# A seven-product down-projection whose combined weights are all prepared during the up-projection

## The chip, the cores and the metric

The kernel runs on one core of a Trainium2 chip. The metric is the device time of one execution in microseconds (us). In the text PE is TensorE, ACT ScalarE, DVE VectorE, POOL GpSimd, and SP the engine that issues most DMAs.

## The reference

One layer of a diffusion backbone over 2048 tokens of width D = 1024 (batch 1): a mixer (an FNet branch and a gated recurrence, merged and projected), then a gated feed-forward network with a 3x3 depthwise convolution, then a final RMS norm. All is float32. The part that matters here is the feed-forward network, D_FF = 2816, on a grid of 32 rows by 64 columns:

```python
def conv_ffn(h, w_up, conv_w, conv_b, w_down, rows, cols):
    z = (h @ w_up).reshape(b, rows, cols, 2 * D_FF)
    z = lax.conv_general_dilated(z, conv_w, ..., padding='SAME', feature_group_count=2 * D_FF)
    z = z.reshape(b, l, 2 * D_FF) + conv_b
    return (jax.nn.silu(z[..., :D_FF]) * z[..., D_FF:]) @ w_down
...
x = x + mx[:, :, 5] * conv_ffn(h2, ffn_up, ffn_conv_w, ffn_conv_b, ffn_down, rows, GRID_W)
return rmsnorm(x, final_g)
```

## The kernel before

Every float32 product is made of three matmuls in the type fp32r: each operand is split into a high part (a cast on ACT, line 102) and a low part (operand minus high part, on POOL or DVE, line 103), and high x high, high x low and low x high are added in PSUM. `split` does this for a tile, and all splits carry the lines 102 and 103, so tiles tell them apart.

The program is written as one stream; a scheduler puts the instructions of each engine in an order, and each engine works through its own in that order. `tc.issue_after(x)` makes what is issued within it stand behind x. A tile pool with `bufs=n` gives a tile name n buffers; the next use of a buffer waits until its last reader is done.

**Up-projection** (1656 to 2687 us of the profile). `NF` = 22 pairs of column blocks, so 44 iterations, counted by jt = 2j + half. Each loads and splits its block of `ffn_up` (`load_w`, tile w_up), and makes 96 matmuls into z, a 128 x 2048 tile in PSUM; two z tiles (za, zb), which take turns, fill the PSUM. Then ACT makes the convolution's centre (line 1031) and a scaled copy `be` (line 1034), on odd iterations also the Silu (line 1036); DVE makes seven taps of the convolution (line 1063, reading z, which it frees at its end); POOL adds `be` (line 1039), and on odd iterations multiplies by the gate (line 1048); SP stores the result as dZ.

**Down-projection** (from 2687 us). The 2816 rows of `w_down` and the output's 2 x 2 blocks (halves of tokens, halves of columns) are treated as a 2 x 2 by 2 x 2 block product, done with seven products in place of eight. `PRODUCTS` says for each which one or two blocks of tokens (dZ), and which one or two of weights, are added or subtracted to make its operands, and to which output quarters the result is added. Each product has KH = 11 steps; a step needs a token operand g (128 x 1024, split in two) and a weight operand w (128 x 512, split), and makes 8 x 3 matmuls. `operand(idx)`, called AHEAD = 5 steps before the step's use, loads and prepares them: token blocks into rg, sum on DVE (line 1132), split into g; weight blocks into rv, sum on DVE (line 1136), split into w. At a product's end its last steps are done accumulator by accumulator, and each accumulator is added by DVE to its quarters of x (`evict`, line 1212). The g tiles and the quarters of x live in slots H0 to H7.

Two kinds of work for the down-projection are written into the up-projection: `gated_weights` (22 times: ffn_down times the gate vector m5, on POOL, line 1071, stored as dV) at jt 4 to 25, and `first_weights` (11 times: the weight operands of the first product; combined on POOL, line 1079, split from ws into wsr, a single buffer, and stored as dW, line 1082) at jt 28 to 38. These are places in the program's text; nothing ties them to the engines' work of those iterations. In the profile the instructions of line 1082 lie between 1826 and 1917 us. The weights of the other six products are loaded from dV, combined and split during the down-projection.

Of the kernel before, what the change touches and what calls it, by code (L numbers as in the profile page):

```python
# [26 lines left out]
P = 128  # L27
# [67 lines left out]
class Layer:  # L95
# [79 lines left out]
    def scratch(self):  # L175
# [15 lines left out]
        self.dW = [dr.tile([P, 2, TB], F32R, name=f"dW{k}") for k in range(KH)]  # L191
# [807 lines left out]
    def phase3(self, p5):  # L999
# [3 lines left out]
        self.m5 = p5.tile([P, D], F32, name="m5")  # L1003
        nc.sync.dma_start(self.m5, self.dm5)
        for j in range(NF):
            acc = []
            for half in range(2):
                jj = j + half * NF
                wh, wl = self.load_w(a["ffn_up"][0, :, jj * P:(jj + 1) * P], f"up{jj}")
                if jj == NF:  # L1010
                    self.psB.__exit__(None, None, None)
                    self.psB = tc.tile_pool(name="ps2b", bufs=1, reuse_waits="tile", space=PSUM)
                    self.zb = self.psB.__enter__()
# [8 lines left out]
                if 4 <= jt < 4 + NF:  # L1022
                    self.gated_weights(p5, jt - 4)
                elif 28 <= jt < 28 + KH:
                    self.first_weights(p5, jt - 28)
# [6 lines left out]
                if not end:  # L1032
                    be = p5.tile([P, SEQ], F32, name="be", tag="be", bufs=2)
                    nc.scalar.activation(be, z, AF.Copy, scale=self.cw[:, 7, jj:jj + 1])  # L1034
# [3 lines left out]
                if not end:  # L1038
                    nc.gpsimd.tensor_tensor(ac[:, :SEQ - 64], ac[:, :SEQ - 64], be[:, 64:], op=ADD)  # L1039
# [25 lines left out]

    def gated_weights(self, p5, k):
# [7 lines left out]
    def first_weights(self, p5, k):  # L1074

        nc = self.nc
        raw = p5.tile([P, 2, TB], F32, name="ws", tag="ws", bufs=2)
        self.load_terms(raw, self.weight_terms(PRODUCTS[0], k))
        nc.gpsimd.tensor_tensor(raw[:, 1, :], raw[:, 1, :], raw[:, 0, :], op=SUB)
        w = p5.tile([P, 2, TB], F32R, name="wsr", tag="wsr", bufs=1)  # L1080
        self.split(w[:, 0, :], w[:, 1, :], raw[:, 1, :])
        nc.gpsimd.dma_start(self.dW[k], w)
# [21 lines left out]
    def weight_terms(self, prod, k):  # L1104
        return [self.dV5[KH * r + k][:, c * TB:(c + 1) * TB] for r, c, _ in prod[1]]

    def load_terms(self, t, terms):

        for q, src in zip((1, 0), terms):
            self.nc.sync.dma_start(t[:, q, :], src)  # L1110

    def operand(self, idx):
# [4 lines left out]
        prod = PRODUCTS[p]  # L1117
        q = idx - 8
        if q % 2 == 0:
            tag = "H2" if q == 0 else "H1" if q == 2 else ("H3", "H6", "H7", "H2")[(q // 2 - 2) % 4]  # L1120
# [3 lines left out]
        rg = self.p6.tile([P, 2, 2 * TB], F32, name="rg", tag="rg", bufs=3)  # L1124
        self.load_terms(rg, [self.dZ[KH * kh + k][:, 2 * th * TB:2 * (th + 1) * TB] for th, kh, _ in prod[0]])
        if p == 0:
            nc.gpsimd.dma_start(w, self.dW[k])
        else:
            rw = self.p6.tile([P, 2, TB], F32, name="rv", tag="rv", bufs=3)
            self.load_terms(rw, self.weight_terms(prod, k))  # L1130
        if len(prod[0]) == 2:
            nc.vector.tensor_tensor(rg[:, 1, :], rg[:, 1, :], rg[:, 0, :], op=prod[0][1][2])  # L1132
        self.split(g[:, 0, :], g[:, 1, :], rg[:, 1, :])
        if p:
            if len(prod[1]) == 2:
                nc.vector.tensor_tensor(rw[:, 1, :], rw[:, 1, :], rw[:, 0, :], op=prod[1][1][2])
            self.split(w[:, 0, :], w[:, 1, :], rw[:, 1, :])
# [11 lines left out]
    def down(self, last, pools):  # L1149
# [4 lines left out]
        with ExitStack() as es:  # L1154
# [27 lines left out]
            def store(th, c, i):  # L1182
                ti = 8 * th + i
                nc.sync.dma_start(self.out[ti * P:(ti + 1) * P, c * TB:(c + 1) * TB], X[th, c][:, i, :])
# [43 lines left out]
            load_quarter(0, 1, "H4")  # L1228
            load_quarter(1, 1, "H5")
# [4 lines left out]
            for p in range(7):  # L1234
                if p == 1:
# [3 lines left out]
                    load_quarter(1, 0, "H0")  # L1239
                if p == 3:  # L1240
                    load_quarter(0, 0, "H1")
# [56 lines left out]
```

## Time and profile before

| | |
|---|---|
| median of 3 runs | 3155.48 us (3154.66 to 3157.67) |
| profiled execution | 3153.45 us, its span 3151.7 us |
| granted TensorE clock, mean | 0.985 |
| matmuls on PE | 14,691 |
| busy share of PE, DVE, ACT, POOL | 96%, 60%, 29%, 35% |

The span runs from the first to the last instruction of the profiled execution; the execution's own time has 1.75 us around it. Rows of instructions in order of time read: start, duration, engine, line, operation, output and inputs, and in brackets how long the engine had been idle and which instruction or DMA it waited for. A row of waits reads: engine, tile and line that waited, what it waited for, total us, times, longest. Rows of a line's or a tile's instructions give the shortest, median and longest duration in ns. A row with a bar gives busy us and the mean ns of one, and then the idle time before.

### The profile page before, as it was taken

To read this page: it belongs to the slowest core of one execution; us is meant where nothing else is said; L and a number is where in the kernel's file an instruction comes from. 1 tells how busy PE (TensorE), PEld (TensorE's weight loads), DVE (VectorE), ACT (ScalarE), POOL (GpSimd) and SP (SyncE) were. 2 spreads that over 40 slices of the span, in tenths; PEclk is the share of its full clock that TensorE was granted. 3 is DMA by queue.
4 is the path that set the end of the run, shared out by engine and by line. 5 is a ranking of instruction groups with operands and counts; after the bars stand their busy time and mean duration, and the time that the engine had idled before them with its cause. 6 is when DMAs were issued, how large, how long until landed. Compare 5 with 4: busy or idle time off the path is not lost. (4 is left out here: it accounts for less than half of the span.)

```text
span 3151.7 us, 38316 instructions
## 1 busy us (share of the span) xinstructions
PE 3029.1 (96%) x14691; PEld 2514.3 (80%) x14691; DVE 1901.9 (60%) x2492; ACT 924.1 (29%) x1439; POOL 1110.4 (35%) x593
## 2 busy tenths in 40 slices
PE   8999999999999999999999868999999999999998
PEld 5977788888888888877887657888888888788876
DVE  6355543566666630376656546777777777666477
ACT  5322111233333322243433122222222223232233
POOL 2200110000000001443345754444434444687763
PEclk9999999999999999999999989999999999999999
DMA  6255644333233222656555542111111111988674
GB/s 249 87 170 184 192 158 147 135 108 107 93 99 113 92 94 92 205 188 210 179 173 180 200 158 83 54 47 54 46 42 54 47 54 58 345 278 285 210 262 144
DMA packets 295449, 447.02 MB, mean 142 GB/s; under 512 B 22155, under 2 KB 160226, under 8 KB 290914
## 3 DMA queue, kind: packets, MB, share of 16 engines
q1 hardware_dynamic: 291906, 432.97, 41.2%
q0 software_dynamic: 3360, 11.60, 1.0%
q8 instruction: 116, 1.90, 0.2%
q14 instruction: 67, 0.55, 0.1%
HBM read 329.92 MB, written 114.56 MB: 141 GB/s over the span
## 5 line engine op out<-in xcount | busy, mean ns | idle before, releaser
L1063 DVE SCALAR_TENSOR_TENSOR ac<-z,cw,ac 128x1953 f32<-128x1953 f32 (+2 forms) x309 | 703.0, 2275 | 322.9 <-ACT be L1034 290.3
L146 PE MATMUL z<-h,w_up 128*128 128x512 f32 x1408 | 553.0, 393 | 44.6 <-DVE ac L1063 39.6
L148 PE MATMUL z<-h,w_up 128*128 128x512 f32 x1408 | 552.0, 392 | 10.3 <-POOL w_up L103 10.1
L147 PE MATMUL z<-h,w_up 128*128 128x512 f32 x1408 | 552.0, 392 | 0.0
L146 PEld LDWEIGHTS z<-h,w_up 128*128 128x128 f32 x1408 | 266.9, 190 | 101.6 <-ACT wsr L102 29.8
L148 PEld LDWEIGHTS z<-h,w_up 128*128 128x128 f32 x1408 | 266.8, 189 | 67.5 <-POOL w_up L103 11.7
L1039 POOL TENSOR_TENSOR ac<-ac,be 128x1984 f32<-128x1984 f32 x43 | 192.1, 4467 | 363.4 <-DVE ac L1063 363.4
L147 PEld LDWEIGHTS z<-h,w_up 128*128 128x128 f32 x1408 | 266.9, 190 | 55.4
L1031 ACT ACTIVATE ac<-z,vt,cw 128x2048 f32<-128x2048 f32 x44 | 90.9, 2065 | 609.8 <-PE z L148 609.8
L1145 PE MATMUL d<-w,g 128*128 128x512 f32 x528 | 211.1, 400 | 5.0 <-DVE x L1212 4.8
L1146 PE MATMUL d<-w,g 128*128 128x512 f32 x528 | 210.5, 399 | 3.4 <-POOL w L103 3.4
L1147 PE MATMUL d<-w,g 128*128 128x512 f32 x528 | 210.1, 398 | 0.0
L103 POOL TENSOR_TENSOR g<-rg,g 128x1024 fp32r<-128x1024 f32 x69 | 183.1, 2665 | 61.9 <-ACT g L102 61.8
L493 ACT ACTIVATE ev<-pj 128x512 f32<-128x512 f32 (+1 forms) x136 | 79.8, 587 | 368.1 <-PE pj L148 337.6
L1132 DVE TENSOR_TENSOR rg<-rg 128x1024 f32<-128x1024 f32 x55 | 97.1, 1768 | 79.7 <-DMA rg<-dZ 75.9
L103 POOL TENSOR_TENSOR w_up<-rw,w_up 128x512 fp32r<-128x512 f32 x88 | 112.5, 1300 | 76.1 <-ACT w_up L102 76.1
L787 PEld LDWEIGHTS pa<-bQ,bkc 128*128 128x128 f32 x896 | 120.7, 191 | 16.6 <-issue 10.3
L103 POOL TENSOR_TENSOR wab<-rw,wab 128x512 fp32r<-128x512 f32 x64 | 93.8, 1485 | 111.4 <-ACT wab L102 111.4
L103 POOL TENSOR_TENSOR w<-rv,w 128x512 fp32r<-128x512 f32 x66 | 108.5, 1648 | 57.8 <-ACT w L102 54.8
L787 PE MATMUL pa<-bQ,bkc 128*128 128x128 f32 x896 | 127.4, 286 | 1.1
L1145 PEld LDWEIGHTS d<-w,g 128*128 128x128 f32 x528 | 100.4, 190 | 32.0 <-DVE x L1212 4.6
L793 DVE COPY_PREDICATED bA<-mask,pa 128x512 f32<-128x512 uint8 x112 | 82.6, 738 | 71.2 <-PE pa L787 70.2
(343 smaller groups left out, 6650.3 us busy)
## 6 DMA issues: line engine op xcount, KB each, us to landing
rg<-dZ SPq DMA_DIRECT2D x124, 512.0 KB, 5.7
rv<-dV SPq DMA_DIRECT2D x110, 256.0 KB, 5.1
rw<-in_ffn_up_dram SPq DMA_DIRECT2D x88, 256.0 KB, 3.6
dZ<-ac SPq DMA_DIRECT2D x22, 1024.0 KB, 4.4
rw<-in_w_in_dram SPq DMA_DIRECT2D x72, 256.0 KB, 3.4
maw<-in_ada_w_dram SPq DMA_DIRECT2D x64, 256.0 KB, 3.1
rw<-in_w_out_dram SPq DMA_DIRECT2D x64, 256.0 KB, 2.6
ws<-in_ffn_down_dram SPq DMA_DIRECT2D x22, 512.0 KB, 4.1
```

What stands on the lines that cost most here:

```text
L103: (eng or self.nc.gpsimd).tensor_tensor(lo, raw, hi, op=SUB)
L146: self.nc.tensor.matmul(ps, lh, rh, start=start and i == 0, stop=False)
L147: self.nc.tensor.matmul(ps, lh, rl, start=False, stop=False)
L148: mm = self.nc.tensor.matmul(ps, ll, rh, start=False, stop=stop and i == last)
L787: mm = nc.tensor.matmul(pa[:, c], kc[:, c], fap(Q, w * P, [(2 * m, nw), (W + m, 2), (1, m)]), start=True, stop=True)
L1031: self.centre = nc.scalar.activation(ac, z, AF.Identity, scale=self.cw[:, 4, jj:jj + 1], bias=self.v("cb", jj))
L1039: nc.gpsimd.tensor_tensor(ac[:, :SEQ - 64], ac[:, :SEQ - 64], be[:, 64:], op=ADD)
L1063: nc.vector.scalar_tensor_tensor(o, z3[:, r0 + dy:r1 + dy, c0 + dx:c1 + dx], self.cw[:, k, jj:jj + 1], o, op0=MUL, op1=ADD)
L1132: nc.vector.tensor_tensor(rg[:, 1, :], rg[:, 1, :], rg[:, 0, :], op=prod[0][1][2])
L1145: nc.tensor.matmul(acc, gh[:, t], wh, start=(k == 0), stop=False)
L1146: nc.tensor.matmul(acc, gh[:, t], wl, start=False, stop=False)
L1147: nc.tensor.matmul(acc, gl[:, t], wh, start=False, stop=(k == KH - 1))
```

## The change

All 77 weight operands of the seven products are combined, split and stored as dW during the up-projection (`split_weights`), and the down-projection loads them ready. `weight_steps` spreads them: eleven iterations with two gated weights each, then 77 split weights over 30 iterations, two or three each. Within `issue_after` these steps stand behind the loads of the iteration's up-weights (SP), behind the `be` activation (ACT) and behind the add (POOL) of given iterations. The buffer m5 shares the two buffers of wsr, and is no longer used when the first split weight needs it.

In the down-projection the raw token blocks have tiles of their own (r0 with four buffers, r1 with three, in place of rg with three buffers of two blocks each); where the operand has two terms, its low part is made by DVE, which makes the sum too. The first four g tiles and the quarters of x swap slots. The stores of the output's second half of tokens are issued by ACT.

```diff
-        self.dW = [dr.tile([P, 2, TB], F32R, name=f"dW{k}") for k in range(KH)]
+        self.dW = [dr.tile([P, 2, TB], F32R, name=f"dW{k}") for k in range(7 * KH)]
...
-        self.m5 = p5.tile([P, D], F32, name="m5")
+        self.paces = []
+        self.m5 = p5.tile([P, D], F32, name="m5", tag="wsr", bufs=2)
...
                 wh, wl = self.load_w(a["ffn_up"][0, :, jj * P:(jj + 1) * P], f"up{jj}")
+                self.weight_steps(p5, 2 * j + half - 2)
...
-                if 4 <= jt < 4 + NF:
-                    self.gated_weights(p5, jt - 4)
-                elif 28 <= jt < 28 + KH:
-                    self.first_weights(p5, jt - 28)
...
-                    nc.scalar.activation(be, z, AF.Copy, scale=self.cw[:, 7, jj:jj + 1])
+                    scaled = nc.scalar.activation(be, z, AF.Copy, scale=self.cw[:, 7, jj:jj + 1])
...
-                    nc.gpsimd.tensor_tensor(ac[:, :SEQ - 64], ac[:, :SEQ - 64], be[:, 64:], op=ADD)
+                    added = nc.gpsimd.tensor_tensor(ac[:, :SEQ - 64], ac[:, :SEQ - 64], be[:, 64:], op=ADD)
+                    self.paces.append((scaled, added))
...
+    def weight_steps(self, p5, jt):
+        if not 0 <= jt < 41:
+            return
+        tc = self.tc
+        with tc.issue_after(self.last_load.ins), tc.issue_after(self.paces[jt + 1][0].ins), tc.issue_after(self.paces[jt][1].ins):
+            if jt < KH:
+                self.gated_weights(p5, jt)
+                self.gated_weights(p5, jt + KH)
+            for idx in range(7 * KH):
+                if KH + idx * 30 // (7 * KH) == jt:
+                    self.split_weights(p5, idx)
...
-    def first_weights(self, p5, k):
+    def split_weights(self, p5, idx):
         nc = self.nc
+        p, k = divmod(idx, KH)
+        terms = PRODUCTS[p][1]
         raw = p5.tile([P, 2, TB], F32, name="ws", tag="ws", bufs=2)
-        self.load_terms(raw, self.weight_terms(PRODUCTS[0], k))
-        nc.gpsimd.tensor_tensor(raw[:, 1, :], raw[:, 1, :], raw[:, 0, :], op=SUB)
-        w = p5.tile([P, 2, TB], F32R, name="wsr", tag="wsr", bufs=1)
+        for q, (r, c, _) in zip((1, 0), terms):
+            nc.sync.dma_start(raw[:, q, :], self.dV5[KH * r + k][:, c * TB:(c + 1) * TB])
+        if len(terms) == 2:
+            nc.gpsimd.tensor_tensor(raw[:, 1, :], raw[:, 1, :], raw[:, 0, :], op=terms[1][2])
+        w = p5.tile([P, 2, TB], F32R, name="wsr", tag="wsr", bufs=2)
         self.split(w[:, 0, :], w[:, 1, :], raw[:, 1, :])
-        nc.gpsimd.dma_start(self.dW[k], w)
+        nc.gpsimd.dma_start(self.dW[idx], w)
...
         q = idx - 8
         if q % 2 == 0:
-            tag = "H2" if q == 0 else "H1" if q == 2 else ("H3", "H6", "H7", "H2")[(q // 2 - 2) % 4]
+            tag = ("H4", "H5")[q // 2] if q < 4 else ("H2", "H3", "H6", "H7")[(q // 2 - 2) % 4]
...
-        rg = self.p6.tile([P, 2, 2 * TB], F32, name="rg", tag="rg", bufs=3)
-        self.load_terms(rg, [self.dZ[KH * kh + k][:, 2 * th * TB:2 * (th + 1) * TB] for th, kh, _ in prod[0]])
-        if p == 0:
-            nc.gpsimd.dma_start(w, self.dW[k])
-        else:
-            rw = self.p6.tile([P, 2, TB], F32, name="rv", tag="rv", bufs=3)
-            self.load_terms(rw, self.weight_terms(prod, k))
-        if len(prod[0]) == 2:
-            nc.vector.tensor_tensor(rg[:, 1, :], rg[:, 1, :], rg[:, 0, :], op=prod[0][1][2])
-        self.split(g[:, 0, :], g[:, 1, :], rg[:, 1, :])
-        if p:
-            if len(prod[1]) == 2:
-                nc.vector.tensor_tensor(rw[:, 1, :], rw[:, 1, :], rw[:, 0, :], op=prod[1][1][2])
-            self.split(w[:, 0, :], w[:, 1, :], rw[:, 1, :])
+        raw = [self.p6.tile([P, 2 * TB], F32, name=f"r{i}", tag=f"r{i}", bufs=4 - i) for i in range(len(terms))]
+        for r, (th, kh, _) in zip(raw, terms):
+            nc.sync.dma_start(r, self.dZ[KH * kh + k][:, 2 * th * TB:2 * (th + 1) * TB])
+        nc.gpsimd.dma_start(w, self.dW[idx])
+        if len(terms) == 2:
+            nc.vector.tensor_tensor(raw[0], raw[0], raw[1], op=terms[1][2])
+        self.split(g[:, 0, :], g[:, 1, :], raw[0], nc.vector if len(terms) == 2 else None)
...
-                nc.sync.dma_start(self.out[...], X[th, c][:, i, :])
+                (nc.scalar if th else nc.sync).dma_start(self.out[...], X[th, c][:, i, :])
...
-            load_quarter(0, 1, "H4")
-            load_quarter(1, 1, "H5")
+            load_quarter(0, 1, "H0")
+            load_quarter(1, 1, "H1")
...
-                    load_quarter(1, 0, "H0")
+                    load_quarter(1, 0, "H4")
                 if p == 3:
-                    load_quarter(0, 0, "H1")
+                    load_quarter(0, 0, "H5")
```

The lines of the changed kernel are: centre 1029, be 1032, Silu 1034, add 1037, gate 1047, combination of split weights 1096, store of dW 1099, token sum 1138, eviction 1214.

What this does to the order of the engines is seen at three places. ACT, in the up-projection, where the combined weights begin; the casts of wsr are those of combined weights, those of w_up belong to the up-projection. Before:

```order
L1034 ACTIVATE be<-z,cw 128x2048
L102 CAST w_up_14963<-rw 128x512 x2
L102 CAST wsr<-ws 128x512 x2
L1031 ACTIVATE ac<-z,vt,cw 128x2048
L1034 ACTIVATE be<-z,cw 128x2048
L1036 ACTIVATE ac<-ac 128x2048
L102 CAST w_up_15085<-rw 128x512 x2
L102 CAST wsr<-ws 128x512 x4
L1031 ACTIVATE ac<-z,vt,cw 128x2048
```

ACT, a like place after the change:

```order
L1029 ACTIVATE ac<-z,vt,cw 128x2048
L1032 ACTIVATE be<-z,cw 128x2048
L1034 ACTIVATE ac<-ac 128x2048
L102 CAST wsr<-ws 128x512 x2
L102 CAST w_up_16510<-rw 128x512 x2
L102 CAST wsr<-ws 128x512
L1029 ACTIVATE ac<-z,vt,cw 128x2048
```

Two or four casts of wsr stood between one iteration's activations and the next centre, in an early part of the phase; now there are two or three in every one of the thirty iterations, the last of them behind the casts of w_up.

POOL, in the same part of the up-projection. Before:

```order
L1071 TENSOR_TENSOR ws<-ws,m_14232 128x1024 x4
L1039 TENSOR_TENSOR ac<-ac,be 128x1984
L1048 TENSOR_TENSOR ac<-ac 128x2048
L1071 TENSOR_TENSOR ws<-ws,m_14232 128x1024 x2
L103 TENSOR_TENSOR w_up_14963<-rw,w_up_14963 128x512 x2
L1079 TENSOR_TENSOR ws<-ws 128x512
L103 TENSOR_TENSOR wsr<-ws,wsr 128x512
L1079 TENSOR_TENSOR ws<-ws 128x512
L1082 DMA dW_297<-wsr 128x1024
```

POOL after the change, one gate-less iteration with three split weights:

```order
L1037 TENSOR_TENSOR ac<-ac,be 128x1984
L1096 TENSOR_TENSOR ws<-ws 128x512 x2
L103 TENSOR_TENSOR wsr<-ws,wsr 128x512 x2
L1099 DMA dW_305<-wsr 128x1024
L1099 DMA dW_306<-wsr 128x1024
L1096 TENSOR_TENSOR ws<-ws 128x512
L103 TENSOR_TENSOR w_up_16510<-rw,w_up_16510 128x512 x2
L103 TENSOR_TENSOR wsr<-ws,wsr 128x512
L1099 DMA dW_307<-wsr 128x1024
L1037 TENSOR_TENSOR ac<-ac,be 128x1984
```

Up to four gated weights stood in a row between two adds; now a fixed set stands between two adds, with the low parts of w_up near its end.

DVE at the entry of the down-projection, where the first product's accumulators (dn) are added to x. Before:

```order
L1132 TENSOR_TENSOR rg<-rg 128x1024
L1212 TENSOR_TENSOR x_19865<-x_19865,dn 128x512
L1136 TENSOR_TENSOR rv<-rv 128x512
L1212 TENSOR_TENSOR x_19874<-x_19874,dn 128x512
L1212 TENSOR_TENSOR x_19865<-x_19865,dn 128x512
L1212 TENSOR_TENSOR x_19874<-x_19874,dn 128x512
L1132 TENSOR_TENSOR rg<-rg 128x1024
L1212 TENSOR_TENSOR x_19865<-x_19865,dn 128x512
L1136 TENSOR_TENSOR rv<-rv 128x512
```

After:

```order
L1214 TENSOR_TENSOR x_20407<-x_20407,dn 128x512
L1214 TENSOR_TENSOR x_20416<-x_20416,dn 128x512
L1138 TENSOR_TENSOR r_20523<-r_20523,r_20524 128x1024
L1214 TENSOR_TENSOR x_20407<-x_20407,dn 128x512
L1214 TENSOR_TENSOR x_20416<-x_20416,dn 128x512
L103 TENSOR_TENSOR g_20397<-r_20523,g_20397 128x1024
L1138 TENSOR_TENSOR r_20557<-r_20557,r_20558 128x1024
L1214 TENSOR_TENSOR x_20407<-x_20407,dn 128x512
L1214 TENSOR_TENSOR x_20416<-x_20416,dn 128x512
```

Token sums and weight sums stood among the evictions; now token sums and low parts of g (line 103) do, and stand later in the row of evictions.

More of the change, by code (lines that the diff above doesn't have):

```diff
@@ L1102, in first_operands @@
             nc.gpsimd.dma_start(self.e_w[:, k % 4], self.dW[k])
[L1104 to L1110, printed above, removed]
     def operand(self, idx):
@@ L1116, in operand @@
         p, k = divmod(idx, KH)
-        prod = PRODUCTS[p]
+        terms = PRODUCTS[p][0]
         q = idx - 8
         if q % 2 == 0:
-            tag = "H2" if q == 0 else "H1" if q == 2 else ("H3", "H6", "H7", "H2")[(q // 2 - 2) % 4]
+            tag = ("H4", "H5")[q // 2] if q < 4 else ("H2", "H3", "H6", "H7")[(q // 2 - 2) % 4]
             self.g2 = self.ph.tile([P, 2, 2, 2 * TB], F32R, name=f"g{q}", tag=tag)
@@ L1183, in store @@
                 ti = 8 * th + i
-                nc.sync.dma_start(self.out[ti * P:(ti + 1) * P, c * TB:(c + 1) * TB], X[th, c][:, i, :])
+                (nc.scalar if th else nc.sync).dma_start(self.out[ti * P:(ti + 1) * P, c * TB:(c + 1) * TB], X[th, c][:, i, :])
             def half_done(i):
```

## The prediction

> **What bounds the kernel now.** I read the page first, then stretches of equal length over the whole program, the waits in the stretches that fell short, and there the instructions in order of time.
>
> ```profile
> PE 3029.1 (96%) x14691; PEld 2514.3 (80%) x14691; DVE 1901.9 (60%) x2492; ACT 924.1 (29%) x1439; POOL 1110.4 (35%) x593
> ```
>
> TensorE (PE) is busy nearly always, and the change leaves its 14,691 matmuls and their order alone. So only places where PE pauses, or runs at a lower granted clock, can pay. The up-projection runs from 1656 to 2687 us; its short stretches, 47 us each, are these, with PE's busy time and starts first, and the granted clock third from the end:
>
> ```profile
> core 0: us, PE busy (x) PEld busy (x) DVE busy (x) ACT busy (x) POOL busy (x), PEclk, DMA share, GB/s
> ...
> 1744.00:1791.00 47.00, 41.95 (x174) 33.51 (x174) 29.92 (x14) 11.92 (x9) 28.59 (x13) 0.93 0.60 203
> 1791.00:1838.00 47.00, 33.99 (x142) 27.32 (x140) 7.67 (x4) 5.06 (x4) 31.47 (x16) 0.89 0.50 173
> 1838.00:1885.00 47.00, 23.77 (x96) 19.20 (x96) 27.58 (x13) 10.79 (x12) 30.66 (x22) 0.77 0.48 154
> 1885.00:1932.00 47.00, 33.46 (x124) 26.98 (x125) 27.33 (x13) 14.10 (x13) 26.74 (x16) 0.80 0.31 98
> 1932.00:1979.00 47.00, 47.00 (x209) 38.89 (x209) 28.64 (x14) 11.70 (x9) 20.81 (x10) 1.00 0.20 65
> ```
>
> A full stretch holds 209 matmuls at clock 1.00; the four short ones hold 174 + 142 + 96 + 124 = 536 instead of 836. The 300 missing, at 47/209 us each, are **67.5 us**, the lower clock (0.77 to 0.93) included. The waits from 1735 to 1950 name the cause (total, times, longest, in us):
>
> ```profile
> DVE ac L1063 <- ACT be L1034: 75.0, 4, 39.3
> ACT wsr L102 <- DMA dW<-wsr: 63.7, 9, 8.8
> ...
> PE z L146 <- DVE ac L1063: 39.6, 3, 17.6
> ...
> ACT wsr L102 <- POOL ws L1079: 38.1, 1, 38.1
> ```
>
> In order of time it reads so:
>
> ```profile
> 1823.55 0.62 ACT L102 CAST wsr<-ws 128x512 fp32r<-128x512 f32 x1 [38.13 <-POOL ws L1079]
> 1831.96 0.62 ACT L102 CAST wsr<-ws 128x512 fp32r<-128x512 f32 x1 [7.79 <-DMA dW<-wsr]
> 1832.48 2.06 ACT L1031 ACTIVATE ac<-z,vt,cw 128x2048 f32<-128x2048 f32 x1
> ...
> 1836.48 16.14 DVE L1063 SCALAR_TENSOR_TENSOR ac<-z,cw,ac 128x2016 f32<-128x2016 f32 x7 [39.26 <-ACT be L1034]
> ...
> 1852.77 0.77 PE L146 MATMUL z<-h,w_up 128*128 128x512 f32 x1 [17.64 <-DVE ac L1063]
> ```
>
> The casts of the first eleven combined weights stand in ACT's queue ahead of the up-projection's own activations. Each waits for its operand, then for the one wsr buffer's store to land. The centre activation behind them is late, the convolution on VectorE (DVE) follows it, and PE waits for the PSUM that the convolution frees. That is a queue-order fault, and pacing removes it.
>
> An undisturbed period of the same phase (one iteration, 2034.85 to 2056.47, 21.6 us):
>
> ```profile
> 2034.85 2.07 ACT L1031 ACTIVATE ac<-z,vt,cw 128x2048 f32<-128x2048 f32 x1 [16.94 <-PE z L148]
> 2056.47 2.07 ACT L1031 ACTIVATE ac<-z,vt,cw 128x2048 f32<-128x2048 f32 x1 [14.87 <-PE z L148]
> 2038.86 16.14 DVE L1063 SCALAR_TENSOR_TENSOR ac<-z,cw,ac 128x2016 f32<-128x2016 f32 x7 [5.81 <-ACT be L1034]
> 2055.15 4.47 POOL L1039 TENSOR_TENSOR ac<-ac,be 128x1984 f32<-128x1984 f32 x1 [11.45 <-DVE ac L1063]
> 2059.70 4.63 POOL L1048 TENSOR_TENSOR ac<-ac 128x2048 f32<-128x2048 f32 x1
> 2064.28 2.55 POOL L103 TENSOR_TENSOR w_up<-rw,w_up 128x512 fp32r<-128x512 f32 x2
> ```
>
> The convolution ends at 2055.0, 1.5 us before PE needs its PSUM: whatever makes the centre over 1.5 us late stops PE. ACT idles about 15 us and POOL about 10 us in a period; there the new work must fit.
>
> The down-projection, in stretches of 26 us (full: 114 starts):
>
> ```profile
> 2737.00:2763.00 26.00, 19.98 (x71) 14.87 (x70) 21.68 (x26) 7.81 (x10) 18.95 (x9) 0.87 1.02 388
> 2763.00:2789.00 26.00, 26.00 (x114) 21.08 (x113) 22.20 (x10) 7.60 (x10) 26.00 (x12) 1.00 0.84 282
> ...
> 3049.00:3075.00 26.00, 21.87 (x83) 16.66 (x83) 14.13 (x18) 7.92 (x15) 19.83 (x9) 0.87 1.01 373
> 3075.00:3101.00 26.00, 25.39 (x107) 19.67 (x107) 26.00 (x29) 9.84 (x17) 16.27 (x8) 1.00 0.70 243
> 3101.00:3127.00 26.00, 22.60 (x87) 17.59 (x86) 16.27 (x40) 6.75 (x12) 10.35 (x6) 0.87 0.06 22
> ```
>
> At 26/114 = 0.228 us a start, the entry (first product to second) lacks 114 - 71 = 43, **9.8 us**; the passage from the sixth product to the seventh (31 + 7 = 38) **8.7 us**; the end 27, **6.2 us**. Together 24.7. The waits of the down-projection name the engine at each of the three:
>
> ```profile
> PE dn L1145 <- DVE x L1212: 6.0, 3, 3.5
> PE d L1145 <- DVE x L1212: 4.8, 5, 3.6
> PE d L1146 <- POOL w L103: 3.4, 2, 2.6
> ```
>
> At the first two, evictions on DVE come late, because sums of later operands stand between them; at the end PE awaits the low part of a weight.
>
> **The change part by part.** *Pacing of the gated weights and of the first product's weights.* The order of ACT and POOL now puts them behind the scale activation and the add of given iterations, so no cast can hold a centre that is already due: -67.5 us. Prices of the paced steps:
>
> ```profile
> 1825.50 1.29 POOL L1079 TENSOR_TENSOR ws<-ws 128x512 f32<-128x512 f32 x1
> ...
> L1082 POOL DMA_DIRECT2D dW<-wsr x11: 571/573/627, 1826.7 to 1916.9; - x11
> ...
> DMA to landing us min/median/max: 2.9/5.1/5.7
> ...
> L1071 POOL TENSOR_TENSOR ws<-ws,m 128x1024 f32<-128x1024 f32 x22 | 52.5, 2400 | 39.6 <-DMA ws<-in_ffn_down_dram 34.5 <-issue 5.1
> ...
> DMA to landing us min/median/max: 3.5/5.7/9.7
> ```
>
> (The first landing is that of the dW stores, the last that of the rg loads, which run while the transfers are at their busiest.) Two gated weights in each of eleven periods are 4.8 us of POOL, below its idle 10.
>
> *66 more split weights in 30 periods* (44 combinations on POOL, 66 casts on ACT, 66 low parts and stores on POOL, 110 loads of ws on SP). A two-term step costs POOL 1.29 for the combination, 1.29 (the same shape) for the low part and 0.3 + 0.57 for the store, 3.45 us; it costs ACT 0.62. Three such steps beside the period's own 4.47 + 2.55 are 17.4 us. With the gate (4.63) they are 22.0, just over 21.6, but that holds in 4 periods only; the other gated ones have a one-term step or two steps (at most 20.7), and the deficit of 0.4 is made up in the next, gate-less period. What matters is the order within a period, counted from the centre: the previous add ends at 3.1; two combinations to 5.7; casts; low parts 6.5 to 9.1; stores issued to 10.6; the third combination 12.3 to 13.6; the third cast waits for the first store (9.4 + 0.6 + 5.1) and ends near 15.8; its low part and store end at 18.3, before the next add at 20.3. ACT is then free 5.8 us before the next centre. With gate and three steps (9 periods) everything is some 3.8 us later: the cast ends at 19.6, 2 us ahead, and POOL ends 1.6 us after the add is due, which delays the add alone, and no one on PE waits for that add within the period. If the landings grow to 9.7, the cast is 4.6 later, 2.0 of it covered by its lead and 1.5 by the convolution's: 1.1 us in 9 periods, 10, and with the lower clock after each pause (67.5 lost where the waits of PE named above and two smaller ones make 54.6) some 12. Below nothing it cannot go, as full stretches are full already. By the stores' own row, the nearest, it is nothing; for the stores' 11 rows being few I take **+2** between 0 and 12. SP gets 110 loads and loses none it needs there: the up-projection's weights come about 12 us ahead of use. DMA had a share of 0.20 in the undisturbed stretch.
>
> *Down, removed.* 44 sums on DVE, 66 casts on ACT, 66 low parts on POOL, 110 loads of 256 KB; 66 ready pairs of 512 KB are loaded from POOL's queue instead. *Moved:* 55 low parts from POOL to DVE, behind their sums. Prices on DVE:
>
> ```profile
> L1132 DVE TENSOR_TENSOR rg<-rg x55: 1210/1586/3425, 2729.3 to 3105.5; 128x1024 f32<-128x1024 f32 x55
> ...
> L1132 DVE TENSOR_TENSOR rg<-rg 128x1024 f32<-128x1024 f32 x55 | 97.1, 1768 | 79.7 <-DMA rg<-dZ 75.9 <-POOL g L103 3.6
> ...
> L1212 DVE TENSOR_TENSOR x<-x,d x80: 671/674/690, 2809.3 to 3143.4; 128x512 f32<-128x512 f32 x80
> ...
> L1199 DVE SCALAR_TENSOR_TENSOR x<-x,rs_y,fg x16: 739/744/2896, 3018.5 to 3040.7; 128x512 f32<-128x512 f32 x16
> ...
> L905 DVE TENSOR_TENSOR ml<-gt,mh x32: 677/852/1376, 1288.2 to 1616.1; 128x512 fp32r<-128x512 f32 x32
> ```
>
> A sum takes 1.21 us at least and 1.59 in the median; evictions, which read PSUM, never stretch. The low part on DVE writes fp32r: the nearest row, half the size, is 0.68 to 1.38, so twice that, 1.35 to 2.75, bounds it with 1.21 below; beside no low parts on POOL I take 1.21 to 1.35. The heaviest product is the sixth: 22 sums and low parts (26.6 us), 16 evictions (10.8), 16 scalings (11.9) are 49.3 of the 264 x 26/114 = 60.2 us that PE needs. At the median 1.59 it is 57.7, still under; at 1.77 each the mean of today's 55, 61.6 would make DVE the bound. I lean to the low end, since of the 135 low parts on POOL in this phase 14 remain, none in this product.
>
> The Trainium skill ("SBUF — State Buffer", section "Who interferes with whom") says that a DVE instruction with two SBUF inputs contends with a GpSimd instruction that reads SBUF, and one with at most one SBUF input outside the two-port modes does not. The trace agrees: 1210 to 3425 for the sums beside POOL, 671 to 690 for evictions with PSUM. By it the sums and low parts run at the low end, and DVE has 11 us to spare in the sixth product; at today's mean it is 1.4 over, evictions come as late as now, and the sum without the gain at that passage is 3079.
>
> *Entry.* DVE's order is now eviction pairs with one sum and one low part between, where a weight sum stood before, so no shorter by itself. The quarters of x go to H0 and H1, so their 16 loads issue after the operand of step 12 instead of ahead of step 8's, into DMAs that are full there (share 1.02); by my walk the ninth lands about when the first evictions are due. Lower end: loss gone (0); upper end: evictions some 4 us later than today, 14. I take half of today's: **-9.8 + 5**.
>
> *Sixth to seventh product.* Today's loss starts with a late load behind POOL's backlog; the backlog goes. The raw buffers (four and three) are refilled only after the low part on DVE. Bounds 0 and 10; I take **-8.7 + 2**.
>
> *End.* Today the last low part of a weight on POOL is waited for; now the weight is loaded. Bounds 0 and today's 6.2; I take **-6.2 + 0**. The tail after the last matmul keeps its work. The stores of half the rows go from SP to ACT, where casts queue behind them; each waits for its scaling on DVE. ACT is busy at most 9.8 of 26 us there, which hides it; without that cover the operands of the seventh product would be late, which the bound of 10 above holds.
>
> **Sum:** -67.5 + 2 - 9.8 + 5 - 8.7 + 2 - 6.2 + 0 = -83.2. The profiled execution took 3153.45, 2.0 less than the median: 3070.3 on its own time, **3072** as a median.
>
> **The rivals.** *(1) Down gives nothing:* DVE becomes the bound of the sixth and seventh product, or the x loads come late at the entry. For it: the 5 us of spare at the median price and the loads' later start. Against: POOL's contention goes. The 17.7 us counted there are lost: 3090, and up to 3095 if the entry loses 14, the passage 10 and the end its 6.2 (30.2 where my sum leaves 7).
>
> *(2) Landings stretch,* the third cast holds the centre in the 9 long periods: the upper end of 12 instead of 2, 3082, and as much again, 3092, if the stalls also push POOL's steps into the next period. For it: wsr has two buffers for three steps, and the wait of 63.7 us shows the same cast waiting for the same store. Against: that was one buffer without pacing, and no dW store took over 5.7.
>
> *(3) Slower than before:* the same wait occurs in all 30 paced periods, since every third step needs the first one's store. It must stop PE for over 83.2/30 = 2.8 us each to eat the gain, so the cast must end 5.8 + 1.5 + 2.8 = 10.1 us later than walked: landings near 15.2. No row of dW stores exceeds 5.7. At 17 it would be 1.8 x 30 = 54 more than that point: 3209.
>
> *(4) More gained:* PE's interval in the products is 0.228 against 0.225 in the up-projection (47/209); if POOL's and DVE's traffic causes that, 1584 x 0.003 = 5, and all terms of mine at their lower ends another 9: 3058.
>
> That the change doesn't do what it says (that the scheduler hoists the steps again) is excluded by the order shown above: the paced rows stand behind be and add.
>
> **How the numbers follow.** Mine 0.64, (1) 0.16, by half lower than I would give it if the sums kept today's mean, (2) 0.10, (4) 0.05, (3) 0.05. The likeliest is 3072. The range takes in (4) at 3058, (1) and (2), and the worst of (1) with (2)'s upper end beside it: 3056 to 3104. Within 0.2%, 6.3 us, a measurement of this kernel cannot tell a change from none, and none of the cases but a mild (3) ends there: same 0.02, slower 0.03, faster 0.95.
>
> **What would show it.** Right: full stretches of 209 from 1697 to 2685 and no wait of PE for the convolution; the third cast's wait for dW under 6 us; sums near 1.21 in the down-projection; entry at 90 starts of 114 or more, and the end without a gap. Wrong: PE waits for DVE's convolution in periods with gate and three steps; DVE busy 26 of 26 in the sixth product; the x loads landing after the first evictions could start.

## The result, and the profile after

The changed kernel takes 3080.48 us in the median of four runs (3078.62 to 3084.41), before it 3155.07: ratio 0.9764, 95% interval 0.9747 to 0.9781, so 74.6 us less. Run again beside other kernels it took 3074.1 (ratio 0.9756, 0.9736 to 0.9775). 3072 was predicted, with 3056 to 3104 as the range.

The page's line of engines, and the four stretches of the up-projection that were short (same columns as before):

```profile
PE 3017.8 (98%) x14691; PEld 2507.9 (82%) x14691; DVE 1847.2 (60%) x2503; ACT 923.0 (30%) x1439; POOL 1065.1 (35%) x714
```

```profile
core 0: us, PE busy (x) PEld busy (x) DVE busy (x) ACT busy (x) POOL busy (x), PEclk, DMA share, GB/s
...
1744.00:1791.00 47.00, 47.00 (x209) 38.93 (x208) 35.31 (x16) 11.69 (x9) 31.28 (x14) 1.00 0.43 153
1791.00:1838.00 47.00, 47.00 (x209) 38.91 (x208) 35.26 (x17) 11.71 (x9) 30.05 (x13) 1.00 0.46 159
1838.00:1885.00 47.00, 47.00 (x209) 38.91 (x208) 35.30 (x16) 11.69 (x9) 28.01 (x11) 1.00 0.47 159
1885.00:1932.00 47.00, 47.00 (x209) 38.93 (x208) 32.15 (x15) 13.09 (x10) 31.14 (x12) 1.00 0.39 135
...
2261.00:2308.00 47.00, 47.00 (x209) 38.93 (x208) 35.30 (x16) 16.07 (x16) 40.51 (x27) 1.00 0.55 179
```

All four are full, at clock 1.00, and so is a stretch in the paced part (2261), where POOL has 40.5 of 47 us of work. From 1700 us on PE waits for nothing in the up-projection any more; these are all its waits, and they lie in the down-projection:

```profile
PE d L1147 <- issue: 3.0, 1, 3.0
PE d L1147 <- DVE x L1214: 2.3, 10, 0.2
PE d L1147 <- ACT g L102: 1.5, 1, 1.5
```

The down-projection's short stretches:

```profile
2678.00:2704.00 26.00, 24.53 (x102) 18.42 (x101) 16.46 (x21) 3.15 (x3) 2.15 (x4) 1.00 1.06 403
...
2808.00:2834.00 26.00, 25.30 (x107) 19.47 (x106) 19.66 (x26) 5.99 (x6) 2.69 (x5) 1.00 0.78 258
...
2990.00:3016.00 26.00, 21.43 (x85) 15.02 (x84) 19.77 (x32) 7.46 (x18) 1.61 (x3) 1.00 0.68 226
```

Against 114 they lack 12, 7 and 29: at 0.228 us 2.7 at the entry, 1.6 at the passage from the third product to the fourth, and 6.6 at the passage from the sixth to the seventh, where 2 were forecast. The gap at the end is gone.

From the starts of the matmuls in each trace I take five numbers: the start of the up-projection (first matmul into z); PE's pauses in it (the time by which two starts of matmuls into z lie further apart than 0.227 us, where they are over 0.3 apart, so that starts 0.43 apart at the halved clock count too; 6.4 us at its very beginning, which all kernels have, are taken off); the down-projection from its first to its last matmul; of that the first product; and the pauses in products six and seven, counted in the same way. Each row has one profile, and the medians are of other executions too.

| kernel | median us | ratio (95%) | up starts | up pauses | down | first product | pauses 6, 7 |
|---|---|---|---|---|---|---|---|
| before | 3155 | 1 | 1656.2 | 66.8 | 454.0 | 70.2 | 14.8 |
| changed | 3080.5 | 0.9764 (0.9747 to 0.9781) | 1662.7 | 0 | 439.3 | 62.7 | 6.8 |
| changed, again | 3074.1 | 0.9756 (0.9736 to 0.9775) | 1651.9 | 0 | 445.0 | 64.5 | 9.1 |
| before, 77 tiles of dW | 3155.7 | 1.0003 (0.9994 to 1.0012) | 1659.2 | 70.8 | 454.0 | 70.2 | 14.0 |
| pacing alone | 3090.9 | 0.9789 (0.9775 to 0.9802) | 1656.6 | 0 | 457.0 | 71.1 | 16.9 |
| changed, unpaced | 3252.4 | 1.0303 (1.0276 to 1.0329) | 1659.2 | 174.1 | 447.7 | 65.4 | 5.7 |
| changed, one wsr | 3137.1 | 0.9940 (0.9924 to 0.9957) | 1652.4 | 59.6 | 447.2 | 66.7 | 8.3 |
| changed, low parts on POOL | 3093.2 | 0.9795 (0.9782 to 0.9808) | 1656.4 | 0 | 455.5 | 64.1 | 12.2 |
| pacing, low parts on DVE | 3075.8 | 0.9744 (0.9731 to 0.9757) | 1656.0 | 0 | 441.8 | 71.4 | 0.6 |
| the same, evictions first | 3075.9 | 0.9746 (0.9733 to 0.9760) | 1659.0 | 0 | 439.4 | 71.5 | 0 |
| changed, slots back | 3089.5 | 0.9785 (0.9771 to 0.9800) | 1656.8 | 0 | 457.3 | 68.8 | 9.1 |
| changed, stores on SP | 3072.0 | 0.9735 (0.9721 to 0.9748) | 1656.8 | 0 | 436.6 | 64.4 | 2.4 |
| changed, evictions first in 7 | 3072.1 | 0.9734 (0.9720 to 0.9747) | 1655.2 | 0 | 437.3 | 64.3 | 0 |
| changed, evictions first | 3062.6 | 0.9705 (0.9688 to 0.9723) | 1650.3 | 0 | 430.8 | 62.9 | 0 |

Between the two profiled executions of the first comparison 74.8 us went: 66.8 in the up-projection's pauses, 14.7 in the down-projection, less 6.4 by which the up-projection began later, less 0.5 in the tail; 0.2 remain by rounding.

### The profile page after: what moved, and what is told of

It is laid out like the page before. It is cut to its first block, busy times and chain, and to the rows that moved or that the text cites. A ratio compares the mean times of both kernels' runs of the same rounds, so it can differ in the third digit from the quotient of the medians.

```text
span 3076.8 us, 38641 instructions
## 1 busy us (share of the span) xinstructions
PE 3017.8 (98%) x14691; PEld 2507.9 (82%) x14691; DVE 1847.2 (60%) x2503; ACT 923.0 (30%) x1439; POOL 1065.1 (35%) x714
## 5 line engine op out<-in xcount | busy, mean ns | idle before, releaser
L102 ACT CAST g<-r 128x1024 fp32r<-128x1024 f32 x69 | 69.9, 1047 | 280.2 <-PE d L1149 113.3
L1136 POOL DMA_DIRECT2D w<-dW x69 | 37.4, 543 | 305.1 <-PE d L1149 275.3
L1138 DVE TENSOR_TENSOR r<-r,r 128x1024 f32<-128x1024 f32 x55 | 68.2, 1242 | 115.3 <-DMA r<-dZ 74.0
L781 ACT COPY bkc<-bK 128x512 f32<-128x512 f32 x112 | 74.2, 663 | 164.1 <-PE pa L787 95.2
```

## The experiments

**Is the later start the change's doing?**

```diff
-        self.dW = [dr.tile([P, 2, TB], F32R, name=f"dW{k}") for k in range(KH)]
+        self.dW = [dr.tile([P, 2, TB], F32R, name=f"dW{k}") for k in range(7 * KH)]
```

> The kernel before with the 77 tiles of dW allocated in memory and only the first eleven used: same instructions in the same order. In the profile of the changed kernel the up-projection begins 6.4 us later than before (1662.65 against 1656.22), although each engine's order is the same up to there. Theory A: the place of the buffers in memory does it; then this kernel is 6 us slower than before, 3161, and its up-projection begins near 1662. Theory B: it differs from run to run; then the time is within 2 us of before and the start lies anywhere from 1656 to 1663.

> The changed kernel once more, unaltered, beside the others of this set. Theory A (the start of the up-projection moves from run to run, 1655 to 1663 in the five profiles so far): its profile shows another start, its median lies within 4 us of 3080. Theory B (something in this kernel makes the earlier phases 6 us longer): its up-projection begins at 1662 again.

The allocation alone makes no difference (1.0003), and the changed kernel, run again, began its up-projection at 1651.9. Over the 14 profiles the start lies anywhere from 1650.3 to 1662.7, with the same order of instructions up to there: theory B of the first and A of the second, though the second's median, 3074.1, is 6 us from 3080 and not within 4. A single pair of profiles can thus differ by 12 us for no reason in the code; differences below that are read from the phase they belong to.

The granted clock goes along with it in part. The first 400 us of the profiles with the latest and the earliest start, the changed kernel and the last of the table (columns as above):

```profile
0.00:400.00 400.00, 373.56 (x2148) 309.84 (x2148) 211.14 (x536) 120.01 (x219) 64.50 (x56) 0.97 0.52 175
```

```profile
0.00:400.00 400.00, 376.31 (x2187) 311.57 (x2188) 212.80 (x543) 120.97 (x221) 65.61 (x56) 0.99 0.53 177
```

Ahead of the up-projection the clock stood at half for 30.7 us in the first and for 6.8 us in the second, and half of the difference, 12.0, is near the 12.4 us between their starts. Over all 14 profiles the two go together only loosely (in the kernel with the slots back it was 27.3 us, with a start at 1656.8), and what lowers the clock is not shown.

**Pacing alone.**

```diff
+                self.weight_steps(p5, 2 * j + half - 2)
...
-                if 4 <= jt < 4 + NF:
-                    self.gated_weights(p5, jt - 4)
-                elif 28 <= jt < 28 + KH:
-                    self.first_weights(p5, jt - 28)
...
+            for k in range(KH):
+                if KH + k * 30 // KH == jt:
+                    self.first_weights(p5, k)
...
-        w = p5.tile([P, 2, TB], F32R, name="wsr", tag="wsr", bufs=1)
+        w = p5.tile([P, 2, TB], F32R, name="wsr", tag="wsr", bufs=2)
```

`weight_steps` has the `issue_after` of the changed kernel, and m5 takes the buffers of wsr here too.

> The kernel before with the pacing alone: the 22 gated weights and the 11 weights of the first product tied to the iterations of the up-projection, with two buffers for wsr; the other 66 weights are combined and split in the down-projection as before. Theory A (the late casts on ACT cost the up-projection 67 us, and the down-projection's 15 us come from its own changes): ratio 0.979, 67 us less, no pause of TensorE in the up-projection, the down-projection as before, 454 us from its first to its last matmul. Rival (part of the 67 us comes back in the down-projection, or was not the pacing): less than 60 us.

64.5 us less than the kernel before, and PE's waits from 1700 us on are those of the down-projection alone:

```profile
PE dn L1157 <- DVE x L1224: 7.0, 3, 4.3
PE d L1157 <- DVE x L1224: 6.9, 5, 5.6
PE d L1158 <- POOL w L103: 3.3, 2, 2.6
```

These are the three waits of before, of like size (6.0, 4.8 and 3.4). Theory A holds: pacing gives the up-projection's 67 us, and nothing in the down-projection. The edit ties the steps, spreads the eleven over 30 iterations and doubles wsr's buffers at once; which of these would do alone was not run.

**Without pacing, and with one wsr buffer.**

```diff
-        with tc.issue_after(self.last_load.ins), tc.issue_after(...), tc.issue_after(...):
+        if True:
```

> The changed kernel without the pacing (the steps are written at the same place, but not tied to the engines' work). ACT's order then has up to seven casts of split weights ahead of a centre, from the first paced iteration on. Theory A (pacing is what recovers the time): PE waits for the convolution again; eleven steps cost 67 us before, so 77 steps with two buffers cost at least as much, 70 to 400 us more than the changed kernel. Rival (the second wsr buffer alone was enough): within 5 us of it.

178 us slower than the changed kernel in the same set (3252.4 against 3074.1). The waits of PE in the up-projection of the unpaced kernel:

```profile
PE z L146 <- DVE ac L1062: 123.1, 13, 17.8
PE z L148 <- POOL w_up L103: 12.3, 3, 10.3
PE z L146 <- ACT w_up L102: 5.1, 1, 5.1
```

The same chain as before, longer. With 77 steps two buffers do not replace the order.

```diff
-        w = p5.tile([P, 2, TB], F32R, name="wsr", tag="wsr", bufs=2)
+        w = p5.tile([P, 2, TB], F32R, name="wsr", tag="wsr", bufs=1)
```

The tile m5, which has the same tag, gets `bufs=1` as well.

> The changed kernel with one wsr buffer instead of two, paced as it is. Each cast then waits for the store of the step before it: cast 0.62, low part 1.29, store 0.57 and 5.9 us to land, 8.4 us a step. By the walk of the prediction the third cast then ends 22.4 us after the centre in a gate-less period of 21.7 and 26 in one with the gate. Theory A (the walk is right, 1.5 us of lateness are free): 3 us in each of 9 periods and some lower clock, 20 to 60 us slower than the changed kernel. Rival (POOL's order hides it, or the stores land sooner): within 5 us.

63 us slower than the changed kernel in the same set, just above the 20 to 60 expected; 59.6 us of it are pauses in the up-projection. The waits of the one-buffer kernel:

```profile
ACT wsr L102 <- DMA dW<-wsr: 303.3, 38, 12.9
...
PE z L146 <- DVE ac L1062: 37.8, 16, 5.0
```

With two buffers the same casts wait too, but each ends before the next centre. The changed kernel's waits and landings, and ACT in order of time:

```profile
ACT wsr L102 <- DMA dW<-wsr: 121.4, 16, 10.1
...
DMA to landing us min/median/max: 3.7/5.9/8.1
```

```profile
2275.11 0.62 ACT L102 CAST wsr<-ws 128x512 fp32r<-128x512 f32 x1 [6.51 <-DMA dW<-wsr]
2278.63 2.07 ACT L1029 ACTIVATE ac<-z,vt,cw 128x2048 f32<-128x2048 f32 x1 [2.90 <-PE z L148]
...
2293.93 0.62 ACT L102 CAST wsr<-ws 128x512 fp32r<-128x512 f32 x1 [7.23 <-DMA dW<-wsr]
2300.39 2.06 ACT L1029 ACTIVATE ac<-z,vt,cw 128x2048 f32<-128x2048 f32 x1 [5.84 <-PE z L148]
```

The third cast waits for the first store, and ACT is then idle 2.9 us before the centre in a period with the gate, 5.8 in one without: the walk had 2.0 and 5.8. Ahead of no centre of the paced part is ACT idle for less than 2.7 us. So the rivals' mechanism is real and the margin small; one buffer less uses it up.

**What gains in the down-projection?** First the low parts back on POOL, the weights still ready:

```diff
-        self.split(g[:, 0, :], g[:, 1, :], raw[0], nc.vector if len(terms) == 2 else None)
+        self.split(g[:, 0, :], g[:, 1, :], raw[0])
```

> The changed kernel with the low parts of two-term tokens back on POOL. Theory A (low parts on POOL stretch the sums on DVE): the sums rise from a mean of 1.24 us to about 1.5, the low parts on POOL take 2.4 or more, and the chain of load, sum, cast and low part becomes 1 to 2 us longer; the passage to the seventh product is later, in all 2 to 8 us slower than the changed kernel. Rival (DVE has the slack and POOL is nearly idle, so it makes no difference): within 2 us of it.

Down takes 455.5 us: ready weights without this move gain next to nothing there against pacing alone (457.0). The sums and the low parts, the changed kernel first, then this one:

```profile
L1138 DVE TENSOR_TENSOR r<-r,r 128x1024 f32<-128x1024 f32 x55 | 68.2, 1242 | 115.3 <-DMA r<-dZ 74.0
...
L103 DVE TENSOR_TENSOR g<-r,g x55: 1211/1218/2987, 2666.9 to 3028.4; 128x1024 fp32r<-128x1024 f32 x55
```

```profile
L1138 DVE TENSOR_TENSOR r<-r,r 128x1024 f32<-128x1024 f32 x55 | 97.4, 1780 | 154.4 <-DMA r<-dZ 132.8 <-issue 10.4 <-POOL g L103 9.1
...
L1138 DVE TENSOR_TENSOR r<-r,r x55: 1209/1226/4145, 2657.7 to 3034.4; 128x1024 f32<-128x1024 f32 x55
...
L103 POOL TENSOR_TENSOR g<-r,g x69: 2378/2402/3728, 2651.1 to 3038.3; 128x1024 fp32r<-128x1024 f32 x69
```

The median stays (1226) and single sums take up to 4145 ns. Of the 55 sums 24 ran while POOL had no TENSOR_TENSOR in work, and none of them took over 1227 ns; the 31 beside one took 2213 in the mean. In the changed kernel only 3 had one beside them. That fits the rule of the Trainium skill that the prediction weighed ("SBUF — State Buffer", "Who interferes with whom"), by which a DVE instruction with two SBUF inputs contends with a GpSimd instruction that reads SBUF. 2 to 8 us were expected; it is 10.5 to 16 in the down-projection against the changed kernel's two profiles. How much of this comes from the stretched sums, and how much from a low part that itself takes 2402 ns on POOL and 1218 on DVE, was not separated.

Then the converse: low parts on DVE, but the weights made in the down-projection as before (on the kernel with pacing alone):

```diff
-        self.split(g[:, 0, :], g[:, 1, :], rg[:, 1, :])
+        self.split(g[:, 0, :], g[:, 1, :], rg[:, 1, :], nc.vector if len(prod[0]) == 2 else None)
```

> The kernel with pacing alone, and the low parts of two-term tokens on DVE; the weights of products 2 to 7 are combined and split in the down-projection, as before. Theory A (ready weights without this move gained nothing in the down-projection, 455.5 against 457.0 us; the move is what gains): the down-projection takes 440 to 448 us, 9 to 17 less than with pacing alone. Rival (both are needed, since DVE then has weight sums, token sums and low parts, and the weights' low parts remain on POOL): 452 us or more.

Theory A: 441.8 us down, 15.2 less than with pacing alone, and a time, 3075.8, like the changed kernel's. The pauses of products six and seven fall from 16.9 to 0.6 us, so the low parts of the tokens on POOL were what made the seventh product late without ready weights; the entry stays as it was:

```profile
PE dn L1157 <- DVE x L1224: 6.8, 3, 3.1
PE d L1157 <- DVE x L1224: 0.9, 4, 0.2
```

So pacing and this one move, on the kernel before, bring what the whole change brings. No run shows a clear gain from the 66 weights moved into the up-projection.

**The slots.**

```diff
-            load_quarter(0, 1, "H0")
-            load_quarter(1, 1, "H1")
+            load_quarter(0, 1, "H4")
+            load_quarter(1, 1, "H5")
```

The first four g tiles and the other two quarters go back to their slots of before too.

> The changed kernel with the first g tiles and the quarters of x in their slots of before. Theory A (the slots have no part in the gain at the entry; that came with the shorter work on DVE and POOL): the first product takes 62 to 65 us and the down-projection 439 to 445, as in the changed kernel. Rival (the swap matters: with the old slots the operands of steps 8 to 11 wait for the first product's tiles): the first product takes 68 to 71 us, 5 us or more slower.

The rival holds: 68.8 us for the first product against 62.7 and 64.5. The entry's gain comes in the main from the swap; with the old slots and no ready weights the first product takes 70.2 to 71.5. Two waits of this kernel:

```profile
ACT g L102 <- PE dn L1149: 19.9, 1, 19.9
...
PE d L1147 <- DVE x L1214: 7.1, 5, 4.9
```

The first, a cast of tokens that waits for matmuls of the first product, is there with the old slots in the kernel before too (19.4 us), and not among the changed kernel's. Sums and low parts that follow it come among the evictions. The third product also became longer (72.1 us against 61.6, PE waiting for evictions up to 4.9 us); why was not tried.

**The passage to the seventh product.** DVE of the changed kernel there, and then PE's pause:

```profile
2985.06 1.23 DVE L1138 TENSOR_TENSOR r<-r,r 128x1024 f32<-128x1024 f32 x1 [6.15 <-issue]
...
2996.29 2.53 DVE L1138 TENSOR_TENSOR r<-r,r 128x1024 f32<-128x1024 f32 x2 [6.16 <-issue]
2998.74 1.22 DVE L103 TENSOR_TENSOR g<-r,g 128x1024 fp32r<-128x1024 f32 x1
2999.87 9.64 DVE L1214 TENSOR_TENSOR x<-x,d 128x512 f32<-128x512 f32 x16
```

```profile
3001.25 0.47 PE L1147 MATMUL d<-w,g 128*128 128x512 f32 x1 [2.97 <-issue]
```

The two sums at 2996.29 stand ahead of the 16 evictions, and DVE was idle 6.2 us before them. By the order they belong to steps 72 and 73, the seventh and eighth of the last product; the program's text has them after the evictions, and the scheduler put them ahead. The loads of their first token blocks were issued at 2989.0 and 2990.2, as the low parts of steps 68 and 69 ended, which free the buffers. Loads of tokens take 7.2 us in the median to land there, so these fit the start at 2996.3.

```diff
-                    if idx + AHEAD < 7 * KH:
+                    if idx + AHEAD < 7 * KH and p < 6:
                         self.operand(idx + AHEAD)
+                    elif idx + AHEAD < 7 * KH:
+                        with tc.issue_after(ev.ins):
+                            self.operand(idx + AHEAD)
```

Here `ev` is the last eviction of the product before.

> The changed kernel with one thing added: the token operands that the text prepares after the sixth product's evictions are queued behind these evictions on DVE too (issue order only). In the changed kernel two sums for them stand ahead of the evictions, wait 6.2 us for their load, and TensorE pauses about 6.5 us (3.4 once, then 0.4 seven times). Theory A (it is the order on DVE): the pause goes, 4 to 6.5 us faster than the changed kernel. Rival (the loads or the low part of step 70 ahead of the evictions keep them late): less than 2 us.

The pauses of products six and seven are gone (0 instead of 6.8 and 9.1), theory A; the total, 3072.1, is 8.4 and 2.0 us below the changed kernel's two medians, which is within what the start's shift allows, so the gain is read from the phase.

> As the kernel that queues the seventh product's operands behind the sixth's evictions, but for all products: each operand prepared during product p stands on DVE behind the evictions of product p - 1. Theory A (sums ahead of evictions also cause the 1.5 to 4.7 us lost at the passage from the third to the fourth product): TensorE's losses there go, the down-projection takes 434 to 436 us from its first to its last matmul in place of 437.3. Rival (what is late there is the loads): no change beyond 1 us against that kernel.

With `p == 0` in place of `p < 6` the passage from the third to the fourth product closes too, and the down-projection takes 430.8 us, lower than expected. PE's waits from 1700 us to the end, all of them:

```profile
PE d L1147 <- ACT g L102: 1.3, 1, 1.3
PE dn L1147 <- DVE x L1214: 0.2, 1, 0.2
```

It is the fastest of all, 3062.6 us, 11.5 less than the changed kernel in the same set. Products two to seven take 61.1 to 61.4 us each.

> The same kernel with the operands of each product queued on DVE behind the evictions of the product before. Theory A (order on DVE is what is left): the down-projection takes 431 to 437 us, and the kernel is within 4 us of the one with ready weights and this order, 3062.6, without the 66 weights in the up-projection. Rival (the weights' work on DVE and POOL keeps the sixth and seventh product late): 440 us or more, 8 us or more slower than that one.

On the kernel with the weights in the down-projection the same edit gives 439.4 us, 2.4 less than without; the total does not move, and neither expectation is met in full: products two to seven take 61.1 to 61.4 us each here too, but the first still takes 71.5 us, for which the slots would have to be swapped. That is the whole difference to 430.8. The combination was not run, so whether the ready weights gain anything stays open.

**The stores.**

```diff
-                (nc.scalar if th else nc.sync).dma_start(self.out[...], X[th, c][:, i, :])
+                nc.sync.dma_start(self.out[...], X[th, c][:, i, :])
```

> The changed kernel with the stores of the output's second half of tokens back on SP. Theory A (they only change the queue; in the sixth product ACT's casts waited up to 14 us behind stores, or else the loads on SP would): within 3 us of the changed kernel, the loss at the passage to the seventh product, 6.8 to 9.1 us in two profiles, between 4 and 12. Rival 1 (stores in SP's queue hold the loads of the seventh product): 5 us or more slower. Rival 2 (ACT's queue was the worse place): 3 us or more faster.

In total (3072.0) it lies 8.5 and 2.1 us below the changed kernel's two medians, which are 6.4 apart themselves, so the total does not decide. The pauses of products six and seven are 2.4 us instead of 6.8 and 9.1, below the 4 to 12 of theory A. Among the waits of the changed kernel stands

```profile
ACT g L102 <- DMA out_dram<-x: 26.2, 2, 14.2
```

which is not among those of this one. In order of time, DVE and then ACT's queue, where the second of the two waits is:

```profile
2972.29 1.23 DVE L1138 TENSOR_TENSOR r<-r,r 128x1024 f32<-128x1024 f32 x1 [6.37 <-DMA r<-dZ]
2973.43 2.07 DVE L1201 SCALAR_TENSOR_TENSOR x<-x,rs_y,fg 128x512 f32<-128x512 f32 x3
```

```profile
2963.30 11.25 ACTq L1186 DMA_DIRECT2D out_dram<-x  x6
2974.59 1.05 ACT L102 CAST g<-r 128x1024 fp32r<-128x1024 f32 x1 [14.22 <-DMA out_dram<-x]
```

A sum waits for its load, three scalings (line 1201) stand behind it on DVE, the sixth store waits for the first of them, and the cast of the seventh product's first tokens, summed at 2957, stands behind that store. That is rival 2 in its mechanism; its 3 us are not shown by the total.

## Why the prediction was right, and where not

- *Pacing, -67.5 + 2.* The sum came out right (66.8, no pauses left), and by its own steps: the cast ahead of the centre had the lead that was walked, and the stores took 5.9 us to land instead of 5.1. The 2 us were not needed. One sign did not hold: the third cast was to wait under 6 us for the store, and the 16 waits are 7.6 in the mean, up to 10.1; ACT came to the cast earlier than walked, and the cast ended in time all the same.
- *DVE's budget.* Sums take 1.24 us in the mean and low parts 1.22 in the median; 1.21 to 1.35 was taken. DVE did not become the bound of the sixth product, whose stretches hold 114 starts. The leaning to the low end was right, and its reason is seen in the low parts put back on POOL: only sums beside work of POOL stretch.
- *Entry, -9.8 + 5.* The step that failed is the bound's reason: the loss left was 2.7 and, with smaller delays, the first product is 7.5 us shorter (5.7 in the second profile), not 4.8, because the swap of slots, which I counted as a cost (later x loads), was what gained. The cost is there, but small: in the second profile evictions waited 2.6 us for loads of x, in the first not at all.
- *Sixth to seventh product, -8.7 + 2.* This step failed in its + 2: 6.8 and 9.1 us of pauses remained, inside the bounds of 0 and 10. The prediction had POOL's backlog as the cause of the late evictions and let it go with POOL's work, and so far it was right (16.9 to 0.6 us by moving the low parts alone). But the changed kernel has a loss of its own there: DVE's order, sums for steps 72 and 73 ahead of the evictions, whose buffers come free only with low parts on DVE, which I had named and put at 2; and ACT's stores ahead of the casts. The stores' move I had called hidden, by ACT's busy time, which says nothing of what a waiting store holds up behind it.
- *End, -6.2.* Right: no pause.
- *What I did not have:* the start of the up-projection moves by up to 12 us from run to run. The first comparison's profile had it 6.4 us late, which is most of the 8.5 by which 3080.5 exceeds 3072; in the second set, with a start at 1651.9, the median was 3074.1.
- *The attribution.* The sum's down-projection part (17.7 forecast, 14.7 measured, 9.0 in the second profile) I gave to the whole of the change there. In the runs the low part on DVE and the swap of slots gain; no clear gain of the ready weights is shown. That the part came out near 17.7 is in part luck: the entry gained more than forecast and the passage to the seventh product less.
- *Rivals.* The mechanism of (2) and (3) exists and is held off by one buffer; stores took up to 8.1 us to land, where (2) and (3) were held against 5.7. Of (1), DVE did not become the bound; the passage kept its loss in part, by the order. (4), a shorter interval in the products, did not happen either: 0.232 us before and after. The 0.228 and 0.225 that it started from are stretches divided by counts which take in the matmul in flight at the edge; from start to start it is 0.232 and 0.227.

## What to carry to other kernels

Work that is ready early goes where the scheduler's order puts it, not where the text has it; tie it to the instruction behind which it may run, and look at what stands ahead of the work on which the bounding engine waits. Before moving work to another phase, try first to move only its one contended instruction to another engine: here one operand of one call gave 15.2 us of the down-projection, as much as the whole change did there (14.7 and 9.0). And a DMA issued from a computing engine's queue holds what stands behind it until it can be issued, however idle that engine looks: here stores held two casts for 26.2 us.

## What was not expected of the hardware

The sums on DVE keep their median beside POOL's low parts (1226 ns) and grow only in the tail, to 4145 ns, so the mean (1780) and not the median says what contention costs. The same program up to the up-projection took 1650.3 to 1662.7 us in 14 profiles, the latest with 30.7 us at half the clock ahead of it and the earliest with 6.8. And a matmul's interval is 0.227 us in the up-projection and in the first eight steps of the down-projection, but 0.232 to 0.233 in the rest, in all kernels, with and without POOL's work; its cause stays open.
